# A mixer and mixture-of-experts block on one core: the low parts of the projections' weights are made on VectorE instead of GpSimd

## The chip, the core and the metric

The kernel runs on one core of one Trainium2 chip. The metric is the device time of one execution in microseconds. The page and the rows below come from one profiled execution. The five engines are named as the profile names them: PE is TensorE (PEld its weight loads), DVE is VectorE, ACT is ScalarE, POOL is GpSimd, SP is SyncE, which here only issues transfers. Each engine takes its own instructions strictly in the order in which the program lists them; an instruction whose input is not there holds everything behind it on that engine.

## The reference, cut to what matters

The block normalises 2048 tokens of width 1024, projects them with one large matrix, runs two recurrent mixers over the projections, mixes their outputs through gates, and ends with a routed mixture of experts.

```python
h = rmsnorm(x, norm1_g[l]) * (1.0 + sc1) + sh1
proj = h @ w_in[l]
hq, hf, hi, hg, rw_p, gates = jnp.split(proj, IN_SPLITS, axis=-1)
o_a = hgrn2_mixer(hq, hf, hi, hg, lb_all[l], hg_norm_g[l])
o_b = rwkv7_mixer(rw_p, ...)
gate_a, gate_b = jnp.split(jax.nn.sigmoid(gates), 2, axis=-1)
mixed = gate_a * (o_a @ w_proj_a[l]) + gate_b * (o_b @ w_proj_b[l])
x = x + gt1 * (mixed @ w_out[l])
...
x = x + gt2 * hier_moe(h2, ...)
return rmsnorm(x, final_g)
```

All is float32. The kernel keeps that accuracy in the large products by splitting each factor into a high part, rounded to the type that TensorE takes in one pass (`FR`), and a low part, which is the remainder; a product is then three matmuls: high by high, high by low and low by high.

## The kernel before, in words

The program has four stages. The first three groups of lines below belong to the stage that the change touches.

- **Projections and mixers (about 46 to 1690 us).** The tokens go in four groups of 512 (`g`). For each group 46 output tiles of 128 columns are projected (`WIN`: 14 of kind rw, 16 hg, 16 gt). A tile takes two weight pieces of 512 rows by 128 columns from `parts`, and 24 matmuls in `win_tiles` (lines 778 to 780: high by high, high by low, low by high for each of eight slices). The result is evicted: rw tiles by ACT (line 783) and then three DVE instructions (785 to 787), hg and gt tiles by ACT or DVE in turn (791, 793), and stored.
- **Pieces.** `parts` does the splitting once. In group 0 a piece is loaded raw (line 759, 256 KB, two buffers `wraw`), its high part is rounded on ACT (760), its low part is the raw piece minus the high part (761), and both are stored to DRAM (763, 512 KB). From group 1 on the finished pair is loaded (756), and lines 759 to 763 are not run. That makes 92 subtractions in group 0. The last 16 run in `mixed` (group 4), for the two output projections of the mixers. The tile `w` has four buffers.
- **Mixers.** They work in 16 blocks of 128 tokens: `rw_prep` of the next block, `rw_chain` and `hg_block` of this one. `rw_prep` has a serial chain of 31 pairs of DVE instructions (lines 243 and 244) that solves a triangular system. Group 0 holds the preparation of blocks 0 to 2, the chains of blocks 0 and 1, and for the next group's tokens the norms and transposes (lines 633 to 657) and two slices of the conditioning matrix (607 to 614). The first 14 tiles of group 0 have hardly any mixer work beside them, since nothing is projected yet.
- **After that** come the output projection, the router and the experts, which the diff does not touch.

A scheduler sets the order on each engine: the program is written block by block, and the scheduler interleaves it by a timeline of its own, taking projection tiles as filling. SP's queue is ordered in the same way; the store of a piece (763) and the next raw load (759) stand in it one behind the other.

Of the kernel before, what the change touches and what calls it, by code (L numbers as in the profile page):

```python
# [6 lines left out]
FP = mybir.dt.float32  # L7
# [4 lines left out]
OP = mybir.AluOpType  # L12
# [738 lines left out]
def parts(k, key, src):  # L751

    nc = k.nc
    w = k.ld.tile([128, 2, 4, 128], FR, name="w", bufs=4)
    if key in k.split:
        nc.sync.dma_start(w.bitcast(FP), k.split[key])
        return w
    raw = k.ld.tile([128, 4, 128], FP, name="wraw", bufs=2)
    nc.sync.dma_start(raw, src.rearrange("(k p) n -> p k n", p=128))
    nc.scalar.copy(w[:, 0], raw)  # L760
    nc.gpsimd.tensor_tensor(w[:, 1], raw, w[:, 0].bitcast(FP), OP.subtract)  # L761
    k.split[key] = k.dr1.tile([128, 2, 4, 128], FP, name="W" + key)
    nc.sync.dma_start(k.split[key], w.bitcast(FP))
    return w


def win_tiles(k, I, hT, g, tiles):

    nc = k.nc
    dst_of = {"rw": k.RWP, "hg": k.HGP, "gt": k.GTP}  # L770
    hi, lo = hT
    for group, ti, c0 in tiles:
        dst = dst_of[group]
        W = [parts(k, f"{group}{ti}_{q}", I['w_in'][0, q * 512:(q + 1) * 512, c0:c0 + 128]) for q in range(2)]
        pt = k.pm.tile([128, 512], FP, name="mm", bufs=3)
        for kk in range(8):
            whi, wlo = (W[kk // 4][:, j, kk % 4] for j in range(2))
            nc.tensor.matmul(pt, whi, hi[kk // 2][:, kk % 2], start=(kk == 0), stop=False)  # L778
            nc.tensor.matmul(pt, whi, lo[kk // 2][:, kk % 2], start=False, stop=False)  # L779
            nc.tensor.matmul(pt, wlo, hi[kk // 2][:, kk % 2], start=False, stop=(kk == 7))  # L780
        ev = k.ld.tile([128, 512], FP, name="ev", bufs=3)
        if group == "rw":
            nc.scalar.activation(ev, pt, AF.Identity, scale=k.omu[:, ti:ti + 1])  # L783
            mu = k.mu[:, ti:ti + 1]; ca = k.carry[:, ti:ti + 1]
            nc.vector.scalar_tensor_tensor(ev[:, 1:512], pt[:, 0:511], mu, ev[:, 1:512], op0=OP.mult, op1=OP.add)  # L785
            nc.vector.scalar_tensor_tensor(ev[:, 0:1], ca, mu, ev[:, 0:1], op0=OP.mult, op1=OP.add)
            nc.vector.tensor_copy(ca, pt[:, 511:512])
        else:
            k.flip ^= 1
            if k.flip:  # L790
                nc.scalar.copy(ev, pt)
            else:
                nc.vector.tensor_copy(ev, pt)
        nc.sync.dma_start(dst[g][ti], ev)
# [46 lines left out]
def mixed(k, I, tiles):  # L841

    nc, ld, ps = k.nc, k.ld, k.pm
    for g, dt in tiles:
        if dt == 0:
            k.mx = load_hT(k, [src[g][m:m + 2] for src in (k.OBT, k.OAT) for m in (0, 2)])
        hi, lo = k.mx
        G = ld.tile([128, 2, 512], FP, name="xin", bufs=k.xb)
        nc.sync.dma_start(G, k.GTP[g].rearrange("(j d) p t -> d p j t", j=2)[dt])
        nc.scalar.activation(G, G, AF.Tanh, scale=0.5)  # L850
        for j, nm in ((1, "w_proj_b"), (0, "w_proj_a")):
            w = parts(k, f"{nm}{dt}", I[nm][0, :, dt * 128:(dt + 1) * 128])
            pt = ps.tile([128, 512], FP, name="mm", bufs=3)
            for kk in range(4):
                o = 4 - j * 4 + kk
                nc.tensor.matmul(pt, w[:, 0, kk], hi[o // 2][:, o % 2], start=(kk == 0), stop=False)  # L856
                nc.tensor.matmul(pt, w[:, 0, kk], lo[o // 2][:, o % 2], start=False, stop=False)  # L857
                nc.tensor.matmul(pt, w[:, 1, kk], hi[o // 2][:, o % 2], start=False, stop=(kk == 3))  # L858
            nc.vector.scalar_tensor_tensor(G[:, j], G[:, j], 1.0, pt, op0=OP.add, op1=OP.mult)
        ev = ld.tile([128, 512], FP, name="ev", bufs=3)  # L860
        nc.gpsimd.tensor_tensor(ev, G[:, 0], G[:, 1], OP.add)
        nc.sync.dma_start(k.MIX[g][dt], ev)
# [661 lines left out]
```

## Time and profile before

| | |
|---|---|
| time, median of 3 runs | 2983.82 us (2966.77 to 2990.27) |
| the profiled execution, its own time | 2984.66 us |
| its span, first to last instruction | 2982.8 us |
| PE busy | 2766.5 us, 93% |
| DVE busy | 1985.8 us, 67% |
| ACT busy | 1286.4 us, 43% |
| POOL busy | 943.0 us, 32% |
| line 761 on POOL | 108 instructions, 145.2 us |

Busy time is an average over stages. The execution's own time is 1.9 us above its span and 0.8 us above the median, so the span's microseconds can be taken as those of the metric.

### The profile page before, as it was taken

What the parts mean: (1) busy time and instruction counts of PE and PEld (TensorE: products, weight loads), DVE (VectorE), ACT (ScalarE), POOL (GpSimd) and SP (SyncE); (2) the same over time, 40 slices, a digit from 0 to 9 for tenths busy, and PEclk for the clock granted to TensorE, in tenths of its full rate; (3) what the DMA queues carried; (4) which work ended last, traced back from release to release, by engine and by line L of the source; (5) the groups of instructions that cost most, each with busy time, mean ns of one, the idle gap of its engine ahead of it and who ended that gap; (6) DMA issues with size and microseconds to landing.
All of it is one profiled execution on the core that took longest, in us unless ns stands there. A gap on an engine that the chain in (4) does not pass through costs nothing. (4 is left out here: it accounts for less than half of the span.)

```text
span 2982.8 us, 45842 instructions
## 1 busy us (share of the span) xinstructions
PE 2766.5 (93%) x15562; PEld 2257.7 (76%) x15562; DVE 1985.8 (67%) x4010; ACT 1286.4 (43%) x2188; POOL 943.0 (32%) x1092
## 2 busy tenths in 40 slices
PE   6989999999999999999999999899959999999992
PEld 4667788887888888888888777788857777777771
DVE  6164666683677666677547876446565798989983
ACT  4332544432343523333233544322224566767772
POOL 3344643322332313342233453332441121112112
PEclk9989999999999999999999989999979999999996
DMA  8897786687565776566555678886448799999996
GB/s 257 285 322 239 224 256 196 196 252 219 174 211 176 232 246 191 180 223 202 187 183 173 187 231 289 302 294 212 142 158 256 264 363 347 363 347 359 373 314 229
DMA packets 460698, 734.65 MB, mean 246 GB/s; under 512 B 115569, under 2 KB 277361, under 8 KB 460354
## 3 DMA queue, kind: packets, MB, share of 16 engines
q1 hardware_dynamic: 448114, 696.68, 69.8%
q0 software_dynamic: 11088, 29.60, 4.3%
q10 hardware_dynamic: 1152, 4.19, 0.4%
q8 instruction: 165, 2.70, 0.4%
q14 instruction: 179, 1.47, 0.1%
HBM read 561.81 MB, written 175.39 MB: 247 GB/s over the span
## 5 line engine op out<-in xcount | busy, mean ns | idle before, releaser
L778 PE MATMUL mm<-hThi,w 128*128 128x512 f32 x1472 | 596.4, 406 | 19.1 <-ACT hThi L667 10.1
L780 PE MATMUL mm<-hThi,w 128*128 128x512 f32 x1472 | 595.4, 405 | 9.2 <-POOL w L761 8.6
L779 PE MATMUL mm<-hTlo,w 128*128 128x512 f32 x1472 | 592.1, 402 | 1.0 <-DVE hTlo L668 0.9
L1206 DVE TENSOR_TENSOR wlo<-raw,whi 128x1024 fp32r<-128x1024 f32 x404 | 484.1, 1254 | 46.1 <-ACT whi L1205 21.5
L1205 ACT CAST whi<-raw 128x1024 fp32r<-128x1024 f32 x408 | 405.7, 1057 | 206.0 <-PE U L931 48.6
L778 PEld LDWEIGHTS mm<-hThi,w 128*128 128x128 f32 x1472 | 282.3, 192 | 88.2 <-ACT hThi L667 10.2
L780 PEld LDWEIGHTS mm<-hThi,w 128*128 128x128 f32 x1472 | 282.0, 192 | 79.5 <-POOL w L761 20.2
L779 PEld LDWEIGHTS mm<-hTlo,w 128*128 128x128 f32 x1472 | 282.1, 192 | 61.2 <-DVE hTlo L668 3.6
L1294 POOL DMA_INDIRECT X<-y,lists x33 | 72.3, 2190 | 497.4 <-DVE y L1292 449.6
L243 DVE TENSOR_TENSOR pr<-Pl,Nl 128x2 f32<-128x2 f32 (+30 forms) x496 | 202.5, 408 | 12.0
L451 POOL TENSOR_TENSOR Xq<-h,kf 128x256 f32<-128x256 f32 x96 | 80.2, 835 | 399.0 <-PE hl L470 116.9
L761 POOL TENSOR_TENSOR w<-wraw,w 128x512 fp32r<-128x512 f32 x108 | 145.2, 1346 | 171.0 <-ACT w L760 153.4
L760 ACT CAST w<-wraw 128x512 fp32r<-128x512 f32 x108 | 66.8, 619 | 152.1 <-DMA wraw<-in_w_in_dram 114.0
L244 DVE TENSOR_REDUCE Pl<-pr 128x1 f32<-128x2 f32 (+30 forms) x496 | 124.0, 250 | 12.0
L856 PE MATMUL mm<-hThi,w 128*128 128x512 f32 x256 | 104.9, 412 | 11.7 <-ACT hThi L667 6.8
L296 PE MATMUL xy<-UV,Gc 128*64 128x64 f32 (+1 forms) x1536 | 114.0, 223 | 0.6 <-ACT UV L305 0.6
L1236 PE MATMUL G<-whi,xh 128*128 128x512 f32 x256 | 104.9, 410 | 9.5 <-PEq L1367 8.3
L296 PEld LDWEIGHTS xy<-UV,Gc 128*64 128x64 f32 (+1 forms) x1536 | 95.6, 127 | 19.4 <-issue 7.1
L857 PE MATMUL mm<-hTlo,w 128*128 128x512 f32 x256 | 105.3, 411 | 2.4 <-DVE hTlo L668 2.4
L785 DVE SCALAR_TENSOR_TENSOR ev<-mm,mu,ev 128x511 f32<-128x511 f32 x56 | 41.8, 747 | 97.1 <-ACT ev L783 93.5
L226 DVE SCALAR_TENSOR_TENSOR Gc<-rp,iv,gmask 128x128 f32<-128x128 f32 x256 | 71.9, 343 | 51.7 <-PE rp L224 51.4
L858 PE MATMUL mm<-hThi,w 128*128 128x512 f32 x256 | 103.8, 406 | 0.0
(492 smaller groups left out, 5924.3 us busy)
## 6 DMA issues: line engine op xcount, KB each, us to landing
raw<-in_exp_w_gate_dram SPq DMA_DIRECT2D x126, 512.0 KB
raw<-in_exp_w_up_dram SPq DMA_DIRECT2D x126, 512.0 KB
raw<-in_exp_w_down_dram SPq DMA_DIRECT2D x124, 512.0 KB
w<-Whg SPq DMA_DIRECT2D x96, 512.0 KB
w<-Wgt SPq DMA_DIRECT2D x96, 512.0 KB
w<-Wrw SPq DMA_DIRECT2D x84, 512.0 KB
wraw<-in_w_in_dram SPq DMA_DIRECT2D x92, 256.0 KB
Whg<-w SPq DMA_DIRECT2D x32, 512.0 KB
```

Source lines behind the costliest of these rows:

```text
L243: nc.vector.tensor_tensor(pv, Pl[:, :ni, :ns], Nl[:, :ns, t_][:, None, :].to_broadcast([128, ni, ns]), OP.mult)
L244: nc.vector.tensor_reduce(Pl[:, :ni, t_], pv, AX.X, OP.add)
L296: mm = lambda *a_, **kw: nc.tensor.matmul(*a_, skip_group_check=True, **kw)
L761: nc.gpsimd.tensor_tensor(w[:, 1], raw, w[:, 0].bitcast(FP), OP.subtract)
L778: nc.tensor.matmul(pt, whi, hi[kk // 2][:, kk % 2], start=(kk == 0), stop=False)
L779: nc.tensor.matmul(pt, whi, lo[kk // 2][:, kk % 2], start=False, stop=False)
L780: nc.tensor.matmul(pt, wlo, hi[kk // 2][:, kk % 2], start=False, stop=(kk == 7))
L856: nc.tensor.matmul(pt, w[:, 0, kk], hi[o // 2][:, o % 2], start=(kk == 0), stop=False)
L857: nc.tensor.matmul(pt, w[:, 0, kk], lo[o // 2][:, o % 2], start=False, stop=False)
L1205: s.nc.scalar.copy(hi, raw)
L1206: eng.tensor_tensor(lo, raw, hi.bitcast(FP), OP.subtract)
L1236: mm = lambda *a, **kw: nc.tensor.matmul(*a, skip_group_check=True, **kw)
```

## The change

The subtraction of line 761 is issued on DVE instead of POOL. Operands and types stay.

```diff
--- before.py
+++ after.py
@@ -758,7 +758,7 @@
     raw = k.ld.tile([128, 4, 128], FP, name="wraw", bufs=2)
     nc.sync.dma_start(raw, src.rearrange("(k p) n -> p k n", p=128))
     nc.scalar.copy(w[:, 0], raw)
-    nc.gpsimd.tensor_tensor(w[:, 1], raw, w[:, 0].bitcast(FP), OP.subtract)
+    nc.vector.tensor_tensor(w[:, 1], raw, w[:, 0].bitcast(FP), OP.subtract)
     k.split[key] = k.dr1.tile([128, 2, 4, 128], FP, name="W" + key)
     nc.sync.dma_start(k.split[key], w.bitcast(FP))
     return w
```

The written order of the program is the same, but the scheduler lists the instructions anew. In the first 435 us and from there on to about the 1600th of the 5184 projection matmuls the lists of all five engines differ in many places; from there to the end of the projections they differ in parts; the order in the expert stage is the same but for a branch's place.

DVE, the first 14 tiles, before: only the three instructions that end an rw tile, tile after tile. `mm` is the product in PSUM, `ev` the evicted tile, `carry` the column that is passed to the next group.

```order
L785 SCALAR_TENSOR_TENSOR ev<-mm,mu,ev 128x511
L786 SCALAR_TENSOR_TENSOR ev<-carry,mu,ev 128x1
L787 COPY carry<-mm 128x1
L785 SCALAR_TENSOR_TENSOR ev<-mm,mu,ev 128x511
L786 SCALAR_TENSOR_TENSOR ev<-carry,mu,ev 128x1
L787 COPY carry<-mm 128x1
L785 SCALAR_TENSOR_TENSOR ev<-mm,mu,ev 128x511
```

DVE at the same place now:

```order
L761 TENSOR_TENSOR w<-wraw,w 128x512 x2
L785 SCALAR_TENSOR_TENSOR ev<-mm,mu,ev 128x511
L786 SCALAR_TENSOR_TENSOR ev<-carry,mu,ev 128x1
L787 COPY carry<-mm 128x1
L761 TENSOR_TENSOR w<-wraw,w 128x512 x2
L785 SCALAR_TENSOR_TENSOR ev<-mm,mu,ev 128x511
L786 SCALAR_TENSOR_TENSOR ev<-carry,mu,ev 128x1
L787 COPY carry<-mm 128x1
L761 TENSOR_TENSOR w<-wraw,w 128x512 x2
```

Two subtractions, those of one later tile's pieces, now stand between the evictions of two tiles. Counted over the list, the eviction of the n-th tile comes behind the subtraction of piece 2n+2; tile n itself uses pieces 2n-1 and 2n.

DVE around the start of the first serial chain, that of `rw_prep` of block 0 (lines 243 and 244), as a piece of the difference; `acc` is a sum of the conditioning vector, `BT` and `bon` belong to the mixer block, `Nl` is the chain's matrix:

```order
+L761 TENSOR_TENSOR w<-wraw,w 128x512
+L260 TENSOR_TENSOR BT<-rp,iv_510 128x512
+L609 SCALAR_TENSOR_TENSOR acc<-xin,cs,acc 128x512 x4
 L280 TENSOR_TENSOR bon<-rp,rwin 128x512
+L761 TENSOR_TENSOR w<-wraw,w 128x512 x2
+L793 COPY ev<-mm 128x512
 L236 MEMSET Nl 128x32
 L243 TENSOR_TENSOR pr<-Pl,Nl 128x2
```

Two subtractions, the 45th and 46th, now stand right ahead of the chain.

DVE further on in the same chain, fifteen pairs of 243 and 244 later:

```order
 L243 TENSOR_TENSOR pr<-Pl,Nl 128x64
 L244 TENSOR_REDUCE Pl<-pr 128x4
+L761 TENSOR_TENSOR w<-wraw,w 128x512
 L243 TENSOR_TENSOR pr<-Pl,Nl 128x68
 L244 TENSOR_REDUCE Pl<-pr 128x4
+L176 TENSOR_SCALAR t_2256<-t_2256 128x512
 L243 TENSOR_TENSOR pr<-Pl,Nl 128x90
-L244 TENSOR_REDUCE Pl<-pr 128x5
+L180 SCALAR_TENSOR_TENSOR t_2284<-rs_458,t_2256 128x128 x3
+L244 TENSOR_REDUCE Pl<-pr 128x5
+L180 SCALAR_TENSOR_TENSOR t_2284<-rs_458,t_2256 128x128
+L761 TENSOR_TENSOR w<-wraw,w 128x512
```

The 47th subtraction comes only here, the 48th with the last row. In the list as a whole 21 subtractions, the 34th to the 54th, lie between the first norm of the next group's tokens in group 0 (line 635) and the reciprocal of block 1's preparation (line 200).

On SP the first 14 tiles now read store, load, store, load, eviction's store, where the eviction's store stood between the two pairs. On POOL the 108 subtractions are gone and the rest keeps nearly its order. At the very start DVE has the first two subtractions ahead of lines 590 and 593, which make the scale and shift that POOL's line 696 needs; before, POOL had them ahead of line 696 itself.

## Rows read from the trace of the kernel before

**Rows 1.** The page, part 1: engine, busy us, share, instructions.

```profile
PE 2766.5 (93%) x15562; PEld 2257.7 (76%) x15562; DVE 1985.8 (67%) x4010; ACT 1286.4 (43%) x2188; POOL 943.0 (32%) x1092
```

**Rows 2.** Windows: length; PE, PEld, DVE, ACT, POOL busy; PE clock; DMA share; GB/s.

```profile
46.00:150.00 104.00, 93.84 (x367) 67.15 (x368) 28.03 (x60) 36.42 (x59) 45.55 (x38) 1.00 0.85 271
150.00:264.00 114.00, 99.58 (x459) 74.98 (x458) 72.31 (x168) 40.00 (x94) 52.47 (x55) 0.88 0.88 284
264.00:434.00 170.00, 164.12 (x997) 132.00 (x995) 102.27 (x245) 73.88 (x140) 91.34 (x99) 0.96 0.79 244
434.00:1680.00 1246.00, 1233.98 (x7994) 1027.39 (x7993) 812.91 (x2039) 453.68 (x926) 378.48 (x528) 0.99 0.65 202
1680.00:1780.00 100.00, 91.09 (x634) 76.70 (x632) 82.25 (x158) 53.99 (x96) 63.53 (x68) 0.91 0.76 236
```

**Rows 3.** Waits of PEld, 60 to 140 us: total, times, longest.

```profile
PEld mm L780 <- POOL w L761: 13.9, 20, 1.1
PEld mm L778 <- ACT w L760: 3.5, 5, 1.4
```

**Rows 4.** Line 761: count; shortest, median, longest ns; first and last start.

```profile
L761 POOL TENSOR_TENSOR w<-wraw,w x108: 1257/1287/2610, 42.0 to 1769.0; 128x512 fp32r<-128x512 f32 x108
```

**Rows 5.** Timeline, one turn of a raw buffer: start, us, engine, instruction.

```profile
84.83 0.39 SPq L759 DMA_DIRECT2D wraw<-in_w_in_dram  x1
88.60 0.62 ACT L760 CAST w<-wraw 128x512 fp32r<-128x512 f32 x1 [1.54 <-DMA wraw<-in_w_in_dram]
89.30 1.29 POOL L761 TENSOR_TENSOR w<-wraw,w 128x512 fp32r<-128x512 f32 x1 [0.88 <-ACT w L760]
91.03 0.39 SPq L759 DMA_DIRECT2D wraw<-in_w_in_dram  x1
```

**Rows 6.** Timeline of DVE: line 785, eleven periods apart.

```profile
70.29 0.75 DVE L785 SCALAR_TENSOR_TENSOR ev<-mm,mu,ev 128x511 f32<-128x511 f32 x1 [4.51 <-ACT ev L783]
142.49 0.75 DVE L785 SCALAR_TENSOR_TENSOR ev<-mm,mu,ev 128x511 f32<-128x511 f32 x1 [5.15 <-ACT ev L783]
```

**Rows 7.** DVE by form, 0 to 440 us: total, mean ns, idle before.

```profile
L207 DVE TENSOR_TENSOR BK<-t,t 128x512 f32<-128x512 f32 x3 | 2.0, 683 | 0.0
L213 DVE TENSOR_TENSOR BK<-t,t 128x512 f32<-128x512 f32 x3 | 4.2, 1389 | 3.4 <-POOL t L212 3.4
```

**Rows 8.** Timelines of POOL and DVE: a subtraction beside a two-input operation.

```profile
213.95 1.26 POOL L761 TENSOR_TENSOR w<-wraw,w 128x512 fp32r<-128x512 f32 x1 [5.51 <-ACT w L760]
214.06 1.20 DVE L243 TENSOR_TENSOR pr<-Pl,Nl 128x14 f32<-128x14 f32 x1
```

**Rows 9.** Window of the DVE work between the 33rd and 54th subtraction's places.

```profile
151.50:241.70 90.20, 77.78 (x358) 59.07 (x359) 66.96 (x157) 35.12 (x86) 41.06 (x44) 0.87 0.90 296
```

**Rows 10.** Timeline of POOL: the 33rd and the 54th subtraction.

```profile
159.22 1.27 POOL L761 TENSOR_TENSOR w<-wraw,w 128x512 fp32r<-128x512 f32 x1 [2.75 <-ACT w L760]
261.20 1.30 POOL L761 TENSOR_TENSOR w<-wraw,w 128x512 fp32r<-128x512 f32 x1 [3.32 <-ACT w L760]
```

**Rows 11.** Timeline of DVE: first and fifteenth pair of the serial chain.

```profile
210.96 0.16 DVE L243 TENSOR_TENSOR pr<-Pl,Nl 128x2 f32<-128x2 f32 x1
220.56 0.22 DVE L244 TENSOR_REDUCE Pl<-pr 128x4 f32<-128x64 f32 x1
```

**Rows 12.** Waits of DVE, 150 to 434 us: total, times, longest.

```profile
DVE BT L260 <- PE rp L258: 13.7, 4, 8.6
DVE Gc L226 <- PE rp L224: 13.6, 5, 6.8
DVE scT L480 <- PE hl L479: 11.0, 4, 4.8
```

**Rows 13.** Timelines of ACT and POOL at the start of the projections.

```profile
42.60 0.62 ACT L760 CAST w<-wraw 128x512 fp32r<-128x512 f32 x1 [0.69 <-DMA wraw<-in_w_in_dram]
41.99 2.57 POOL L761 TENSOR_TENSOR w<-wraw,w 128x512 fp32r<-128x512 f32 x2 [12.01 <-ACT w L760]
44.55 2.82 POOL L696 TENSOR_SCALAR rwin<-rwin,A,mod 128x512 f32<-128x512 f32 x3
```

## The prediction

> **What bounds the kernel now.** I read the page's busy shares first, then the windows by stage, then who waits for the subtraction, then single turns in the timeline. TensorE is busy 93% of the span [rows 1], and from 434 to 1680 us, where no subtraction runs, 1233.98 of 1246 us [rows 2]: that stretch has nothing to give, and the same matmuls run in any order. Slack lies in the first group, where the 92 pieces are made. The reader is to see three stretches in the windows. From 46 to 150 us PE is busy 93.84 of 104 us at full clock, and its weight loads wait 13.9 us for the subtraction and 3.5 us for the rounding in the 80 us from 60 on [rows 3]: there pieces arrive too late. From 150 to 264 us the granted clock is 0.88 and the DMA share 0.88, while DVE is busy 72.31 of 114 us. From 264 to 434 us PE is busy 164.12 of 170 us [rows 2].
>
> **What moves, and its price.** 108 subtractions leave POOL, where one takes 1287 ns at the median [rows 4], 145 us with their mean. On DVE none of this kind is in the trace. The nearest row is a two-input operation of the same 128x512 float32 size, 0.683 us. The upper end is another of that size, 1.389 us, whose mean contains stays beside POOL [rows 7]. I take 0.68 us, since POOL has less to do once its subtractions are gone: 92 x 0.68 = 62.6 us more for DVE in the first group, 73 us in all.
>
> A part of this comes back. A DVE operation on two SBUF inputs that began 0.11 us after a POOL subtraction took 1.20 us and ended 0.05 us behind it, though its row has 14 elements [rows 8]: it stood still until POOL was through. The Trainium skill ("SBUF — State Buffer", "Who interferes with whom") says that a VectorE instruction with two SBUF inputs contends with a GpSimd instruction that reads SBUF and that whichever is second blocks fully. The trace agrees. By that rule the new subtractions are themselves blocked by what is left on POOL, which speaks against the change; the rival on this is priced below.
>
> **First, the start.** POOL's first two subtractions stand ahead of line 696 and end at 44.56 us; 696 begins at 44.55 [rows 13]. Now DVE has them ahead of lines 590 and 593, on which 696 waits. The second rounding ends at 42.60 + 0.62 = 43.22 [rows 13]; with 0.68 us for the subtraction and some 0.4 us for two small instructions (my estimate from the 0.16 us of the smallest DVE rows [rows 11], twice with a gap) 696 begins at 44.3. Gain 0.3 us, near zero either way.
>
> **Second, 46 to 150 us.** One raw buffer's turn is issue 84.83, rounding 88.60, subtraction 89.30, next issue 91.03, that is 6.2 us, 1.29 of them the subtraction [rows 5]. Two buffers serve two pieces per tile, so a turn is about a tile, and eleven tiles take 142.49 - 70.29 = 72.2 us, 6.56 each [rows 6]. A subtraction of 0.68 cuts 0.61 us from each turn if the load lands as fast. That is where the limit may pass on: a tile moves 2 x 256 KB in, 2 x 512 KB and 256 KB out, 1.835 MB. With a DMA share of 0.85 at 271 GB/s [rows 2] a full share would be 319 GB/s, 5.75 us per tile, so at most 0.81 us is to be had, and loads will land later as the share rises. Over 13 tiles: nothing at the low end (loads stretch by as much), 10.5 us at the high end; I take 0.5 us each, 6.5 us. The new order costs nothing here: the eviction of tile n (line 785) comes behind the subtraction of piece 2n+2, which the buffers allow before PE needs it, and SP no longer holds a raw load behind an eviction's store.
>
> **Third, 150 to 264 us.** Here DVE must serve both. Its work between the places of the 33rd and 54th subtraction took 66.96 us of busy time in 90.2 us [rows 9]. With 21 x 0.68 = 14.3 us more it is 81.3 us if all its idle time is filled, 104.5 if all 23.2 us of idle stay. Before, POOL needed 261.20 - 159.22 = 102.0 us for these pieces [rows 10], so the stretch comes out between 2.5 us longer and, since a DMA share of 0.88 leaves 12% [rows 2], 13.7 us shorter. The long gap speaks for the upper part: fifteen pairs of the serial chain without a subtraction, 220.78 - 210.96 = 9.8 us before [rows 11], about 7 without the two blocks by POOL and the two additions in it. Two finished pieces keep PE busy at most a tile's 6.56 us. I allow a cost of up to 8 us and take a gain of 3.
>
> **Fourth, the rest.** From 264 to 434 us 38 subtractions add 25.8 us to DVE's 102.27 of 170 [rows 2], and PE, nearly full, can win 5.9 us at most; I take 0, between a cost of 8 and a gain of 4. In 1680 to 1780 us 16 of them add 10.9 us to DVE's 82.25, which is tight, and take 20.6 us from POOL's 63.53, which relieves the same mixer work [rows 2]; 0, give or take 4. Later evictions and mixer blocks follow the new order with the same matmuls; 0, give or take 4.
>
> **Sum.** 0.3 + 6.5 + 3 = 9.8 us off the profiled execution's 2984.66 us (span 2982.8, and 0.8 above the median of the runs): **2974.9, forecast 2975 us**, 0.3% faster. About 1% is what a measurement of this kernel can tell from no change, so this would read as the same.
>
> **Rivals.**
>
> *The transfers are the limit.* The subtraction ends sooner and the load lands later by as much; the turn stays at 6.56 us per tile. For it: DMA shares of 0.85 and 0.88 in the two stretches. Against it: in [rows 5] 3.77 us pass from issue to rounding for 256 KB, so a load is more than its share of bandwidth. Time 2984, give or take 5.
>
> *DVE holds the pieces back: slower.* In DVE's order a subtraction stands behind instructions that wait for PE, and PE's next projection matmul waits for that subtraction. Before, POOL had almost nothing but subtractions and could not be held so. DVE waited 13.7, 13.6 and 11.0 us for PE in the lines 260, 226 and 480 between 150 and 434 us [rows 12], 38.3 us. It decides from the point where a DVE wait and the work since the last subtraction together pass the 6.56 us that two pieces last. If half of the 38.3 us falls into such gaps, the time is 2984.7 - 6.8 + 19 = 2997; if all of it does, 3016. For it: the 9.8 us gap. Against it: most gaps between neighbouring subtractions are one to four rows of under 0.7 us, and these waits were idle time in which PE had other work.
>
> *POOL blocks the subtraction on DVE.* At 1.389 instead of 0.68 us [rows 7] each costs 0.7 us more; for the 21 in the tight stretch that is 15 us and the gain of the third step is gone and more: 2984.7 - 6.8 + 12 = 2990. This is the rule of the Trainium skill that was named above. Against it: POOL was busy 52.47 of 114 us there, some 27 of them with the 21 subtractions of 1.29 us that leave.
>
> *The clock comes back too.* If pieces arrive in time and the stretch from 150 to 264 us runs at the full level of 2.4 GHz instead of 0.88 of it, 0.12 x 114 = 13.7 us, with 0.04 x 170 = 6.8 us of the next stretch and the high end of the second step: 2984.7 - 0.3 - 10.5 - 13.7 - 6.8 = 2953. Against it: the mixer's own waits lie in the same stretches and stay.
>
> **Chances and range.** Forecast 0.5 (between 2954 and 2981, a little of it below), transfers 0.2, DVE holding 0.15, POOL blocking 0.05, clock 0.1. Faster by over 1% (below 2954): the clock's case and a little of the forecast's, 0.13. Slower by over 1% (above 3013.7): the upper part of the holding case, 0.1. Same 0.77. The range leaves out the clock's lower half and the end of the holding case: 2952 to 3008.
>
> **What would show it.** Line 761 on DVE near 0.7 us, not 1.3. Eleven tiles of line 785 in 66 to 67 us instead of 72.2. The weight loads' wait for 761 between 60 and 140 us down from 13.9 us to a few. DVE up by 60 to 75 us in all, POOL down by about 145. The last piece of group 0 some 10 us before 431, and no change of the distance from there to the end. The prediction is wrong if PE waits for 761 after 150 us longer than before, if tiles still take 6.5 us, or if the difference arises after 440 us, where I put nothing.

## The result and the profile after

The kernel with the subtractions on VectorE took 2962.7 us (median of 20 runs, 2948.4 to 2971.4), the kernel before 2978.8 us beside it (20 runs). The ratio is 0.9941, 95% interval 0.9931 to 0.9952: 0.6% faster, 16 us. That is within the 1% that the text takes for no change (20 runs of each tell more than that: the interval leaves out 1), within the range, and 12 us below the forecast of 2975. Half of these 12 us lie in the start: the forecast was taken off the profiled execution's 2984.66, and over 20 runs the kernel before has 2978.8. The gain itself was forecast as 9.8 us and came out at 16. The profiled execution of the kernel after took 2957.4 us and has a span of 2955.5 us.

The page, part 1, of the kernel after (engine, busy us, share, instructions), beside [rows 1]:

```profile
PE 2750.0 (93%) x15562; PEld 2252.1 (76%) x15562; DVE 2022.0 (68%) x4118; ACT 1277.8 (43%) x2184; POOL 807.6 (27%) x984
```

POOL lost 135 us, DVE gained only 36, though its 108 new instructions take 80.6 us. Line 761 of the kernel after (count; shortest, median, longest ns; first and last start), then what ended DVE's idle time ahead of it:

```profile
L761 DVE TENSOR_TENSOR w<-wraw,w x108: 664/692/1777, 42.7 to 1754.1; 128x512 fp32r<-128x512 f32 x108
...
  ACT w L760: 95.9, 59
```

The subtraction costs DVE 0.69 us at the median where POOL needed 1.287 [rows 4]. The windows after, with the columns of [rows 2]:

```profile
46.00:150.00 104.00, 98.01 (x392) 71.97 (x392) 45.67 (x95) 38.22 (x68) 9.59 (x12) 1.00 0.93 295
150.00:264.00 114.00, 102.73 (x479) 78.68 (x479) 78.58 (x188) 40.26 (x93) 20.96 (x28) 0.94 0.94 301
264.00:434.00 170.00, 163.39 (x1074) 135.15 (x1074) 118.21 (x288) 76.79 (x148) 43.06 (x63) 0.99 0.80 255
434.00:1680.00 1246.00, 1228.74 (x7977) 1023.69 (x7976) 819.62 (x2062) 457.43 (x934) 381.30 (x531) 0.99 0.65 200
1680.00:1780.00 100.00, 95.39 (x621) 79.90 (x621) 82.99 (x174) 48.88 (x85) 47.85 (x54) 0.90 0.78 243
```

Against [rows 2], the first two stretches hold 25 and 20 more matmuls, the third 77 more; the granted clock of 150 to 264 us is 0.94 where it was 0.88, and the DMA share rises from 0.85 and 0.88 to 0.93 and 0.94. The weight loads' waits between 60 and 140 us, beside [rows 3]:

```profile
PEld mm L780 <- DVE w L761: 6.8, 17, 0.6
PEld mm L778 <- ACT w L760: 4.7, 10, 1.5
```

One raw buffer's turn in the timelines of the kernel after, beside [rows 5]: load issued 84.29, rounded from 88.17, subtracted from 88.83, next load of this buffer issued 89.96, 5.67 us where it was 6.20. These are single turns; means over many pieces stand below.

```profile
84.29 0.39 SPq L759 DMA_DIRECT2D wraw<-in_w_in_dram  x1
88.17 0.62 ACT L760 CAST w<-wraw 128x512 fp32r<-128x512 f32 x1 [2.36 <-DMA wraw<-in_w_in_dram]
88.83 0.69 DVE L761 TENSOR_TENSOR w<-wraw,w 128x512 fp32r<-128x512 f32 x1 [2.29 <-ACT w L760]
89.96 0.39 SPq L759 DMA_DIRECT2D wraw<-in_w_in_dram  x1
```

Line 785 at the same two tiles as in [rows 6], from DVE's timeline after: 66.1 us for eleven tiles, 6.01 each, where it was 72.2.

```profile
71.27 0.74 DVE L785 SCALAR_TENSOR_TENSOR ev<-mm,mu,ev 128x511 f32<-128x511 f32 x1
137.39 0.74 DVE L785 SCALAR_TENSOR_TENSOR ev<-mm,mu,ev 128x511 f32<-128x511 f32 x1
```

To say where the rest came from, two marks are needed that were not shown ahead of the prediction: the 30th and the 92nd subtraction, the 92nd being the last of group 0. First POOL's timeline of the kernel before, then DVE's of the kernel after:

```profile
144.15 1.29 POOL L761 TENSOR_TENSOR w<-wraw,w 128x512 fp32r<-128x512 f32 x1 [1.80 <-ACT w L760]
431.64 1.38 POOL L761 TENSOR_TENSOR w<-wraw,w 128x512 fp32r<-128x512 f32 x1 [1.33 <-ACT w L760]
```

```profile
136.78 0.69 DVE L761 TENSOR_TENSOR w<-wraw,w 128x512 fp32r<-128x512 f32 x1 [1.83 <-ACT w L760]
411.21 0.69 DVE L761 TENSOR_TENSOR w<-wraw,w 128x512 fp32r<-128x512 f32 x1
```

Up to the 30th piece 7.4 us were won, from there to the 92nd 13.0 more (287.5 against 274.4), 20.4 in all. Between 760 and 1350 us the mixer's blocks (line 280) of the two profiles stand 10 to 13 us apart, at 1590 us 16 and at 1767 us 19; the two spans differ by 27.3 us, the medians of the runs by 16. So two single executions cannot say to a few us where the gain of the medians arises. What they show is a lead of 20.4 us at the 92nd piece, about half of which is given back by the middle of the span; and the larger part of that lead arises where the prediction had only 3 us: beside the mixers.

### The profile page after: what moved, and what is told of

It reads as the page before. It is cut to its first block, busy times and chain, and to the rows that moved or that the text cites. A ratio compares the mean times of both kernels' runs of the same rounds, so it can differ in the third digit from the quotient of the medians.

```text
span 2955.5 us, 45796 instructions
## 1 busy us (share of the span) xinstructions
PE 2750.0 (93%) x15562; PEld 2252.1 (76%) x15562; DVE 2022.0 (68%) x4118; ACT 1277.8 (43%) x2184; POOL 807.6 (27%) x984
## 5 line engine op out<-in xcount | busy, mean ns | idle before, releaser
L778 PE MATMUL mm<-hThi,w 128*128 128x512 f32 x1472 | 593.2, 403 | 16.5 <-ACT hThi L667 10.3
L1294 POOL DMA_INDIRECT X<-y,lists x33 | 72.2, 2189 | 490.5 <-DVE y L1292 445.6
L243 DVE TENSOR_TENSOR pr<-Pl,Nl 128x2 f32<-128x2 f32 (+30 forms) x496 | 194.7, 393 | 11.7
L761 DVE TENSOR_TENSOR w<-wraw,w 128x512 fp32r<-128x512 f32 x108 | 80.5, 746 | 101.6 <-ACT w L760 95.9
L856 PE MATMUL mm<-hThi,w 128*128 128x512 f32 x256 | 104.3, 410 | 10.3 <-ACT hThi L667 7.6
L1236 PE MATMUL G<-wlo,xh 128*128 128x512 f32 x256 | 101.6, 397 | 0.0
L1236 PE MATMUL G<-whi,xl 128*128 128x512 f32 x256 | 101.6, 397 | 0.0
```

The costliest lines, as they stand in the source:

```text
L243: nc.vector.tensor_tensor(pv, Pl[:, :ni, :ns], Nl[:, :ns, t_][:, None, :].to_broadcast([128, ni, ns]), OP.mult)
L1236: mm = lambda *a, **kw: nc.tensor.matmul(*a, skip_group_check=True, **kw)
```

## Experiments

**The question** was therefore why the stretch from the 30th to the 92nd subtraction (in short: the middle) got 13 us shorter. Three theories. *Turn*: the subtraction is a link in each raw buffer's turn in the middle too, and the shorter link delivers pieces sooner. *Lock*: a subtraction on POOL stops DVE's two-input operations [rows 8], and the mixers' chain no longer pays that; with it goes the variant that POOL's own mixer instructions stood behind the subtractions. *Order*: the list of instructions is laid out anew when one changes its engine, and the new one is better by chance. For lock I worked out DVE's *stays*: for each DVE instruction the time above the duration that a fifth of the instructions of its shape stay under, summed over 144 to 434 us. They are 32.1 us before and 14.5 after, so 17.6 us went away, which fits the 13 us well. It was the theory that I believed.

The table has all kernels with two raw buffers. A turn is the time from one load's issue to the issue of the next load into the same buffer, mean over pieces, from the timelines of SP (line 759), ACT (760) and DVE or POOL (761), the nth of each belonging together; #30 and #92 are starts of those subtractions; stays as above; the ratio is to the kernel before, run beside each group of kernels (its median was 2974.8 to 2980.7 us from group to group, so medians of different groups are compared by their ratios). Turns, marks and stays come from one profiled execution of each kernel.

```
                    turn 7-30  turn 31-90  #30    #92    middle  stays  median   ratio
before                6.54       9.30     144.2  431.6   287.5   32.1   2978.8   1
after                 6.04       8.76     136.8  411.2   274.4   14.5   2962.7   0.9941 (0.9931-0.9952)
e1_rw_only            6.10       9.68     136.6  435.3   298.7   36.5   2989.5   1.0024 (1.001-1.0039)
e2_hg_gt_only         6.49       8.63     143.6  413.9   270.3   13.1   2968.7   0.9943 (0.9928-0.9958)
e3_proj_only           -         9.31     144.1  431.7   287.6   35.0   2980.7   0.9996 (0.9978-1.0013)
e7_twice_dve          6.64       9.36     144.2  431.1   286.9   14.1   2990.3   1.0026 (1.0011-1.004)
e9_pool_work          6.15       9.30     138.2  425.0   286.8   37.0   2969.1   0.9977 (0.9963-0.999)
e10_pool_wait         6.05       8.81     136.9  412.8   275.8   12.8   2972.4   0.9985 (0.9972-0.9999)
e11_pool_reads        6.03       8.83     135.9  412.8   276.9   32.8   2960.9   0.9947 (0.9928-0.9967)
e12_pool_writes       6.03       8.68     136.6  406.5   269.9   16.9   2963.2   0.9955 (0.9935-0.9976)
```

That a short turn and a short middle go together is nearly the same statement twice; what decides is which edit changes the turn.

**Parts of the change.** Three kernels make one part of it each (other pieces stay on POOL):

```diff
-    nc.gpsimd.tensor_tensor(w[:, 1], raw, w[:, 0].bitcast(FP), OP.subtract)
+    (nc.vector if key[:2] == "rw" else nc.gpsimd).tensor_tensor(...)            # e1_rw_only
+    (nc.vector if key[:2] in ("hg", "gt") else nc.gpsimd).tensor_tensor(...)    # e2_hg_gt_only
+    (nc.vector if key[:2] == "w_" else nc.gpsimd).tensor_tensor(...)            # e3_proj_only
```

e1_rw_only, the first 28 pieces. Expected: 

> Only the 28 subtractions of the rw tiles (the first 14 tiles) on DVE, the other 80 on POOL. Theory turn (the subtraction is part of the raw buffer's turn, and the turn sets the tile's period in the first 150 us): eleven tiles in 66 us as in the changed kernel, the 30th subtraction at 137 instead of 144 us, and about 7 us less in all. Theory lock (POOL's subtractions stop DVE's two-input operations and with them the mixers): next to nothing, below 2 us, since the mixers hardly run in that stretch. Theory order (the new list is better by chance, whichever engine subtracts): anything between 15 us less and 10 us more, with no bond to the first stretch.

e2_hg_gt_only, the 64 pieces beside the mixers. Expected: 

> Only the 64 subtractions of the hg and gt tiles on DVE, the rw tiles and the 16 of the output projections on POOL. Turn: the first stretch stays at 72 us for eleven tiles; from there to the end of group 0 some 4 us less, 4 in all. Lock: most of the change's gain, 10 us or more, since this is where the mixers and the subtractions meet. A holding DVE (the rival of the prediction) would show here as a loss.

e3_proj_only, the 16 pieces of the output projections. Expected: 

> Only the 16 subtractions of the two output projections (around 1680 to 1780 us) on DVE. Turn: within 2 us of the kernel before. Lock: 1 to 4 us less, since DVE is busy 82 of 100 us there. Order: a few us either way; the list of the first 1600 us is nearly that of before, so a large difference would say that listing alone moves the time.

The pieces beside the mixers have the whole gain by the ratio (0.9943), the last 16 none (0.9996). For the former turn had forecast 4 us and lock 10 or more; 17 were won by the ratio, 12 by the medians of its group, so this run spoke for lock. The first 28 by themselves win their 7.5 us by the 30th piece, as turn had forecast, and then lose 11 in the middle: 1.0024, a little slower, where turn had 7 us less in all; only the wide range given for order holds this time. In that run the turn of the middle is 9.68 us, 0.38 longer than before; its subtractions on POOL start 0.78 us behind the rounding at the mean instead of 0.59. Why its new list does that to POOL was not settled.

**Twice the subtraction, on DVE.** It writes the same values twice.

```diff
     nc.vector.tensor_tensor(w[:, 1], raw, w[:, 0].bitcast(FP), OP.subtract)
+    nc.vector.tensor_tensor(w[:, 1], raw, w[:, 0].bitcast(FP), OP.subtract)
```

Expected: 

> The changed kernel with each subtraction done twice over on DVE (same result): 75 us more work on DVE, and a turn longer by 0.69 us. Turn: the tile's period in the first stretch goes back from 6.0 to about 6.6 us, eleven tiles in 72 us, and the kernel comes out 8 to 12 us above the changed one, near the kernel before. Lock: no POOL subtraction in it, so the gain should mostly stay, 0 to 5 us above the changed one. If DVE's load in the middle were close to a limit, 20 us or more above it.

Windows of e7_twice_dve, columns as in [rows 2]:

```profile
46.00:150.00 104.00, 93.42 (x366) 67.93 (x367) 62.05 (x118) 36.98 (x60) 9.75 (x10) 1.00 0.85 270
150.00:264.00 114.00, 98.14 (x463) 75.24 (x462) 91.17 (x218) 39.80 (x93) 23.98 (x31) 0.93 0.87 280
264.00:434.00 170.00, 163.40 (x1050) 132.52 (x1049) 137.71 (x325) 74.56 (x145) 45.48 (x61) 0.98 0.81 250
```

POOL is as empty as after the change and DVE's stays are as short (14.1 us), and still both marks stand where they stood before, 144.2 and 431.1. The link from the rounding's end to the subtraction's end became 2.85 us in the middle (before 1.94, after 1.27), the turn 9.36. PE is back at 93.42 and 98.14 us in the first two stretches, within 1.5 us of [rows 2]. The median is even 8 us above the kernel before, by the ratio, and so 25 above the changed one; turn had forecast 8 to 12, and 20 or more was the forecast for a DVE close to its limit. The gain thus hangs on the subtraction's length in the turn, whichever engine has it, or on DVE's free time, which this run took away too (91.17 of 114 us). No run gives DVE as much work outside the turn, so the two are not told apart. The run does settle another point: the granted clock is 0.93 and 0.98 in the two stretches of the middle, as good as after the change (0.94, 0.99), and the middle is as long as before. A better clock alone does not make the gain.

**POOL's load back, without the turn.** e9, e10, e11 and e12 are the changed kernel with something for POOL behind each piece of the 64; the scratch tile is read by nobody.

```diff
# e9_pool_work: reads the finished piece, twice 256 columns
+    lo = w[:, 1].bitcast(FP); 2 x nc.gpsimd.tensor_tensor(scr, lo[:, 0:2], lo[:, 2:4], OP.subtract)
# e10_pool_wait: waits for the rounding as the subtraction did, copies one column
+    nc.gpsimd.tensor_copy(scr, w[:, 0, 0, 0:1].bitcast(FP))
# e11_pool_reads: one column of the finished piece, then work on the scratch tile alone
+    nc.gpsimd.tensor_copy(scr[:, 0:1], w[:, 1, 0, 0:1].bitcast(FP))
+    nc.gpsimd.memset(scr, 0.0); 2 x nc.gpsimd.tensor_tensor(scr, scr, scr, OP.subtract)
# e12_pool_writes: the same place and length, but it only writes
+    nc.gpsimd.tensor_copy(scr[:, 0:1], w[:, 1, 0, 0:1].bitcast(FP)); 6 x nc.gpsimd.memset(scr, 0.0)
```

e9_pool_work. Expected: 

> The changed kernel, and for each piece of the hg and gt tiles POOL gets two additional subtractions of 256 columns, on the finished piece into a scratch tile that nobody reads: together about the 1.29 us that one subtraction took on POOL before. They come behind the subtraction on DVE, so the raw buffer's turn and the piece's readiness are as in the changed kernel; POOL's load, its in-order queue and its reads of SBUF beside DVE are as before the change. Lock or POOL's queue: the stretch from the 30th to the 92nd subtraction goes back from 274 to about 287 us, DVE's mean for two-input operations (line 243) from 393 towards 408 ns, the time to 2972 to 2981 us. Turn: the stretch stays near 274 and the time within 2963 give or take 5. Order by chance: no relation to either, the list is new again.

e10_pool_wait. Expected: 

> The changed kernel, and for each piece of the hg and gt tiles POOL copies one column of the rounded piece into a scratch tile: an instruction of some 0.1 us that makes POOL's queue wait for ACT's rounding where the subtraction made it wait before, without its work. POOL's queue (the mixer's POOL instructions stand behind waits for pieces): the stretch from the 30th to the 92nd subtraction goes back towards 287 us and the time to 2972 to 2981. Lock: POOL does not read enough to stop DVE, so the stretch stays near 274 and the time at 2963 give or take 5. Turn: the same as lock. Order by chance: no relation.

e11_pool_reads. Expected: 

> The changed kernel, and behind each finished piece of the hg and gt tiles POOL copies one column of it, clears a scratch tile of 256 columns and subtracts that tile twice from itself: about 1.7 us of POOL per piece, nearly all of it reading SBUF, and no buffer of the pieces is held by it beyond the one column. Lock: DVE's two-input operations stand still beside it as before the change; DVE's time over its usual durations between 144 and 434 us goes from 14 back to 30 us or more, the stretch from the 30th to the 92nd subtraction to 284 to 290 us, the time to 2968 to 2980. POOL's load (the mixer's POOL instructions stand behind it): the same as in the run with as much POOL work that only writes. Turn: 274 us and no change.

e12_pool_writes. Expected: 

> The same as the run whose POOL work reads, with six clearings of the scratch tile in place of one clearing and two subtractions: as much POOL work per piece (1.7 us) in the same place, but it only writes SBUF. Lock in the form that only a reading POOL instruction stops DVE's two-input operations: DVE's time over its usual durations stays at 14 us, the stretch from the 30th to the 92nd at 272 to 277 us, the time within 6 us of the changed kernel. POOL's load: as in the run whose POOL work reads, 284 to 290 us. A lock that asks only whether POOL works on SBUF: as in that run too, with the DVE time going up.

e9 looked like proof of the lock: stays 37.0 us, the middle back at 286.8, as forecast for lock or POOL's queue. But its POOL instructions read the piece and so keep the piece's buffer, and ACT waited for that. Waits of ACT from 144 to 434 us in e9_pool_work (total, times, longest):

```profile
ACT w L760 <- POOL scr L761: 9.8, 3, 5.3
```

So e11 and e12 keep no more than a column. Windows 150:264 and 264:434 of e11_pool_reads, then of e12_pool_writes:

```profile
150.00:264.00 114.00, 101.70 (x484) 78.12 (x484) 85.47 (x187) 40.78 (x91) 73.62 (x129) 0.93 0.92 294
264.00:434.00 170.00, 162.64 (x1042) 132.89 (x1042) 124.32 (x273) 74.46 (x140) 107.39 (x199) 0.98 0.82 252
```

```profile
150.00:264.00 114.00, 103.76 (x485) 83.35 (x484) 75.61 (x181) 41.59 (x93) 71.38 (x210) 0.93 0.97 313
264.00:434.00 170.00, 163.55 (x1077) 135.35 (x1076) 124.89 (x297) 76.17 (x148) 116.07 (x301) 0.97 0.79 248
```

POOL is fuller in both than before the change (52.47 and 91.34 us [rows 2]); what it was given came to 2.0 and 2.2 us per piece. In e11 the stays of DVE are back in full, 32.8 us, its busy time in 150 to 264 us is 6.9 us over that of the kernel after; and the middle takes 276.9 us, 2.5 more than after, the kernel 2960.9: against a forecast of 284 to 290 and 2968 to 2980 next to nothing is lost. In e12 the stays hardly grow (16.9) and there is no loss either. So with two raw buffers the lock is real and does not explain the 13 us: DVE stands still in time that hardly anybody waits for. The variants fall as well: POOL's load (e11, e12) and its queue's waiting for roundings (e10, middle 275.8, though its copy took 0.64 us at the median instead of the expected 0.1). The Trainium skill ("SBUF — State Buffer", "Who interferes with whom") says that a DVE instruction with two SBUF inputs contends with a GpSimd instruction that reads SBUF and not with one that only writes it; 32.8 us of stays against 16.9 agree.

Two things stay open. In e9 ACT's three waits are 9.8 us of the 12.4 that its middle lost against the kernel after, but e11 and e12 have waits of this kind too (14.3 us in seven and 10.5 in six, none above 3.0) and lose nothing, so it may have been its list. And e10, alike in the middle, took 2972.4 us, which lies in the range forecast for POOL's queue. Its middle, where the queue waits, speaks against that, and it has no new list either: PE, ACT and SP have the same order as in the kernel after from start to end, DVE and POOL but for a few neighbours, and the lead goes bit by bit, all along the projections. What differs in the trace is the pace of the projections: from 434 to 1680 us neighbouring matmuls start 0.233 us apart at the mean, where it is 0.2285 in the kernels before and after and in e9, e11 and e12 (spacings of 0.20 to 0.26 us). Over the 3312 matmuls of the last three groups that would be 15 us, an estimate. Why the matmuls are slower is not shown.

**Order.** The kernels that subtract the 64 pieces once, on DVE, and leave the pieces' buffers nearly alone (after, e2, e10, e11, e12) have the middle at 269.9 to 276.9 us; those that subtract them on POOL (before, e1, e3) have it at 287.5 to 298.7. Apart from e10, which has the list of the kernel after, and e3, which has that of the kernel before up to 1690 us, PE's lists all differ. So one lucky list does not explain the middle, though a list can move it by 11 us (e1).

**A third raw buffer.** It takes the subtraction's length off the turn's account. The 2 KB for it come from line 599's tile, which has to share a buffer: first one of the mixers' (e4b, e5b), then the raw buffers themselves, which lie idle in the later groups (e13, e14).

```diff
-    raw = k.ld.tile([128, 4, 128], FP, name="wraw", bufs=2)
+    raw = k.ld.tile([128, 4, 128], FP, name="wraw", bufs=3)
-    acc = k.wk.tile([128, 512], FP, name="acc")
+    acc = k.wk.tile([128, 512], FP, name="ysq")                                     # e4b, e5b
+    acc = k.ld.tile([128, 4, 128], FP, name="wraw", bufs=3).rearrange("p k n -> p (k n)")   # e13, e14
```

e4b_raw3_pool, subtraction on POOL. Expected: 

> The kernel before, subtraction on POOL, with three raw buffers instead of two (the room comes from line 599's tile, which takes the buffer of line 334's name). Turn: with three buffers the subtraction's length no longer sets when the next load is issued; the tiles of the first stretch come in 6.0 us or less instead of 6.56, the stretch from the 30th to the 92nd goes from 287 towards 274, and the time comes to 2963 to 2969 without any move to DVE. Lock or POOL's queue: the first stretch gets shorter as with the subtraction on DVE, but the stretch from the 30th to the 92nd does not, 287 us or more; 2975 to 2985. Order by chance: no relation.

e5b_raw3_dve, on DVE. Expected: 

> The changed kernel, subtraction on DVE, with three raw buffers instead of two (room as in the run with three on POOL). Turn: what is left of the turn goes as well; the weight loads' wait for the subtraction between 60 and 140 us falls from 6.8 to under 2 us and the time to 2955 to 2961. Lock or POOL's queue: the middle is as in the changed kernel; 2963 give or take 5, the first tiles earlier by up to 4 us and given back by the 92nd. Transfers as the next limit: no change of the tiles' distance of 6.0 us.

e13_raw3_dve, on DVE. Expected: 

> The changed kernel with three raw buffers; the room comes from line 599's tile, which now takes one of the raw buffers' places and no buffer of the mixers. In the earlier run the last piece of group 0 came 30 us sooner (381.6) and all of it was given back between 411 and 1620 us. If the shared mixer buffer gave it back (waits of line 611 for line 609, 19.4 us): the lead at the 92nd subtraction stays and the time is 2930 to 2950. If the mixers are the limit once the projections run ahead: the lead is lost again by the middle of the span, whatever the room; 2965 to 2995.

e14_raw3_pool, on POOL. Expected: 

> Three raw buffers with the room of line 599's tile as in the run beside it, subtraction on POOL. Turn: the tiles of the first stretch come in 5.1 to 5.4 us with POOL too, as in the earlier run with three. Lock: the stretch from the 30th to the 92nd subtraction stays longer than with three buffers and DVE by 10 to 20 us (277.5 against 258.9 in the earlier pair), so moving the subtraction to DVE is worth as much with three buffers as with two; time 10 to 20 us above that of three buffers with DVE.

```
                 #30    #92    stays  median   ratio
e4b_raw3_pool   123.8  401.3   39.9   3021.3   1.0154 (1.0134-1.0175)
e5b_raw3_dve    122.7  381.6   11.9   2993.9   1.0071 (1.0053-1.0089)
e14_raw3_pool   123.7  398.3   40.9   2972.9   0.9987 (0.9969-1.0005)
e13_raw3_dve    122.0  380.2   16.7   2939.8   0.9877 (0.9856-0.9899)
```

Line 785 in e14_raw3_pool, at the tiles of [rows 6], and the window with its DMA share and GB/s:

```profile
72.28 0.75 DVE L785 SCALAR_TENSOR_TENSOR ev<-mm,mu,ev 128x511 f32<-128x511 f32 x1 [3.06 <-ACT ev L783]
...
128.12 0.75 DVE L785 SCALAR_TENSOR_TENSOR ev<-mm,mu,ev 128x511 f32<-128x511 f32 x1 [4.37 <-ACT ev L783]
```

```profile
46.00:150.00 104.00, 97.28 (x424) 79.50 (x424) 32.52 (x71) 44.25 (x82) 56.44 (x50) 0.97 0.97 335
```

With the slow subtraction on POOL, the tiles come 5.08 us apart, closer than with the fast one and two buffers (6.01). So the limit in the first stretch is the turn, not the engine. In the middle e14 takes 274.6 us, as long as the kernel after, with all of POOL's subtractions and 40.9 us of stays: the 13 us can be had without moving the subtraction. Both kernels of the first pair missed their forecasts of time (2963 to 2969 and 2955 to 2961). They lost their lead (e5b's 92nd piece came 30 us ahead of that of the kernel after) behind the 92nd piece, part of it in waits for the shared mixer buffer, here those of PE from 411 to 1620 us in e5b_raw3_dve:

```profile
PE mm L611 <- DVE ysq L609: 19.4, 4, 7.3
```

In e13, which shares another buffer, this wait is gone and most of the lead stays, with the time in the range forecast for that (2930 to 2950). It is the fastest kernel of the study, 1.2% under the kernel before and by the two ratios 0.6% under the changed one. Its waits of the weight loads from 60 to 140 us, and its windows:

```profile
PEld mm L778 <- ACT w L760: 1.1, 1, 1.1
```

```profile
46.00:150.00 104.00, 97.02 (x424) 79.71 (x424) 52.02 (x112) 47.74 (x91) 12.64 (x18) 0.96 1.00 347
150.00:264.00 114.00, 109.09 (x556) 85.88 (x557) 75.48 (x189) 37.57 (x78) 18.37 (x24) 0.97 0.94 307
264.00:434.00 170.00, 168.82 (x1138) 141.34 (x1137) 132.32 (x315) 80.27 (x160) 60.92 (x83) 1.00 0.76 242
```

The waits for the subtraction are gone in that stretch, and PE has 109.09 and 168.82 us in the two stretches of the middle. One expectation of turn fell: with three buffers the engine should hardly matter, yet DVE is 33 us better than POOL (2939.8 against 2972.9), 16.4 of them in the middle. For the middle that is what lock had forecast, 10 to 20 us. Where the loads are no longer late, something on POOL's side may count, stays or the mixers' POOL instructions, or the list; no run tells these apart. What was said against the lock holds for two buffers.

## Why the prediction was right, and where it was not

**Price of the instruction.** 0.68 us was taken from [rows 7]; 0.692 was measured. POOL down by 145: 135. DVE up by 60 to 75: 36, for more than half because stays went away, 17.6 us in the middle and some 8 between 1680 and 1800 us; the text described them with [rows 8] and did not put them into the sum for DVE. The rest was not followed up.

**First, the start.** The first projection matmul began at 46.2 us, before at 46.0. A gain of 0.3 did not show.

**Second, 46 to 150 us: right.** Tiles came 6.01 us apart (6.0 from the sum, 66.1 us for eleven where 66 to 67 was said), the mean turn of the pieces 7 to 30 fell from 6.54 to 6.04, the weight loads' wait for the subtraction from 13.9 to 6.8 us, and the 30th piece came 7.4 us sooner where the sum had 6.5. The loads did land later, by 0.14 us from issue to rounding, so that the 0.60 us that the subtraction lost became 0.50 of the turn, the very figure of the sum. The rival of the transfers falls. Its bound was wrong too: 319 GB/s at full share gave 5.75 us per tile at best, and e14 did 5.08 at a share of 0.97. That part of the gain does not live by itself, though: in e1 it was all there at the 30th piece and gone at the 92nd.

**Third and fourth, from 150 us to the 92nd piece: the terms that were mis-sized.** Said were 3 us up to 264 us, between a cost of 8 and a gain of 13.7, and nothing behind; 13.0 were won from the 30th to the 92nd piece. (The 13.7 took 12% of the window's 114 us; of the 102.0 us of its pieces it would be 12.2.) By its own marks the third step does not look wrong: from the 33rd to the 54th subtraction 102.0 us became 98.3. But single marks are worth little, the lead being 9.0 us at the 32nd piece, 13.3 at the 33rd and 10.3 at the 34th. The step that failed is "Here DVE must serve both": I asked whether DVE had room, and took the gain back for the gap of the serial chain. That the length of the subtraction itself could matter beside the mixers, as in the second step, I did not ask. e7 takes the gain away by nothing but a second subtraction; it lengthens the link and takes DVE's time at once, and since the change itself takes DVE's time and wins, the length is the likelier cause.

How the shorter subtraction becomes 13 us is shown less well. The means fit: of the turn's 0.54 us less, 0.64 are the subtraction (1.35 before, 0.71 after) and 0.10 the way from issue to rounding (5.67, 5.57), the wait of the subtraction behind the rounding is about the same (0.59, 0.56), and 0.22 are lost from the subtraction's end to the next issue (1.07, 1.29). Some 30 turns with 0.54 us are 16 us. But the gain does not come turn by turn. For the pieces 31 to 50 the mean turn fell from 10.26 to 9.51 us, for 51 to 70 from 9.41 to 7.46, three times what the subtraction lost, and for 71 to 90 it rose from 8.22 to 9.30. The lead grows to 37.2 us at the 72nd piece, here before and after, and then shrinks to 20.4:

```profile
349.79 1.74 POOL L761 TENSOR_TENSOR w<-wraw,w 128x512 fp32r<-128x512 f32 x1
```

```profile
312.54 0.68 DVE L761 TENSOR_TENSOR w<-wraw,w 128x512 fp32r<-128x512 f32 x1
```

And the next load follows the subtraction within 0.7 us in only 34 of the 60 turns before and 35 after; in the others it comes later. So the second step's sum does not simply go on to the last piece, and what makes the rest is not shown. SP's queue shows the link where it holds: its waits from 46 to 434 us, first before, then after, are those of the store that stands ahead of the next load.

```profile
SPq L763 <- POOL w L761: 125.5, 63, 5.6
```

```profile
SPq L763 <- DVE w L761: 100.9, 56, 6.4
```

**DVE holds the pieces back.** It did not: the wait behind the rounding is as long on DVE as it was on POOL. What DVE waits for from 150 to 434 us is now the rounding itself, where [rows 12] had PE:

```profile
DVE w L761 <- ACT w L760: 44.8, 28, 4.5
```

So the added work went into idle time, as the text's "Against it" had it. PE does not wait longer for the subtraction behind 150 us either, which the text had named as a sign of being wrong; its weight loads' waits from 150 to 434 us, before and after:

```profile
PEld mm L780 <- POOL w L761: 4.4, 4, 1.4
```

```profile
PEld mm L780 <- DVE w L761: 1.7, 2, 1.4
```

That "POOL had almost nothing but subtractions" was not so: they are some 27 of its 52.47 us from 150 to 264 us, and they waited 0.59 us behind the rounding there too. e7 shows the point from which the work on DVE costs: with 0.7 us more per piece all is lost.

**POOL blocks the subtraction.** 0.746 us at the mean against 0.692 at the median: 6 us over 108 instructions, not the 0.7 us each of the rival. e11, which puts POOL's reads back, lengthens them to 0.81 us in the middle and costs nothing.

**The clock comes back too.** In part: 0.94 instead of 0.88, and 0.99 instead of 0.96 in the next stretch; by the rival's own way of counting 6.8 + 5.1 us, nearly the 13 of the middle. PE's own rows look like it: between the two marks its idle time is the same before and after (20.7 and 21.0 us) and its busy time 13 us shorter; neighbouring projection matmuls that start 0.43 us apart, where 0.23 is usual, were 57 and became 24. But two runs have a better clock without the gain. e7 has 0.93 and 0.98 and 26 such spacings. e3, whose list up to 1690 us is that of the kernel before, has 34 of them and a granted clock of 0.91 from 150 to 264 us instead of 0.88, and its middle takes 287.6 us:

```profile
150.00:264.00 114.00, 95.67 (x460) 72.40 (x459) 74.01 (x168) 39.97 (x94) 51.98 (x55) 0.91 0.89 286
```

So a better clock alone does not shorten the middle. Whether it is a part of the gain, or follows from matmuls that wait less, no run tells.

**The rest.** The distance from the 92nd piece to the end, said to be unchanged, is 4 us longer by the medians (20.4 won, 16 left), within the 4 that were allowed for new lists; in the two profiled executions it is 7 us shorter. The runs of one kernel spread over 23 to 26 us, so neither can be told from chance. The time lies in the forecast's band of 2954 to 2981 us, but only the first stretch's part of it was worked out rightly; that the middle added a gain and no loss is luck as far as the working goes, which had between 8 us lost and 13.7 won there.

## What to carry to other kernels

Where a buffer's turn sets the pace and the next load is issued right behind an instruction, a shorter instruction gives nearly its difference in length for each turn (here 0.55 us per tile for 0.60). Ask for that chain in every stretch, also where other engines look busy, before asking which engine has room; there the gain can be had too, but it does not come turn by turn. Where a turn is the limit, one more buffer gives more than a faster link (5.08 against 6.01 us per tile), but look at whose room it takes: with a mixer's buffer shared the ratio was 1.0071, with a raw buffer shared 0.9877. A stall that the trace shows and that fits the gain in size is no cause yet; put the stall back alone and see whether the time comes back, and do not carry the answer over to another number of buffers.

## What the runs showed that I had not expected

DVE can stand still for 18 us more in 290 us, on an engine that is busy for some 70% of them, and the kernel does not get longer (e11, 0.9947 against 0.9941). The DMA engines moved 335 to 347 GB/s from 46 to 150 us with three raw buffers, where 271 GB/s at a share of 0.85 had suggested 319 as the most. And a kernel with the same order on PE took some 10 us more because its projection matmuls started 0.233 instead of 0.2285 us apart (e10).
